# Gates and branches of a mixer computed token-major, half-width inverse levels, attention scores of two head groups in turn

## Chip, cores, metric

One core of one Trainium2 chip runs the whole program. The metric is the device time of one execution in microseconds (us); lower is better. Nothing is shared with another core.

## The reference, cut to what matters

The input is 256 tokens of 1024 features; two layers follow one another. Each layer is a feed-forward part, a mixer and a second feed-forward part, each with a residual. The mixer projects the normed input by `w_in` into the inputs of three branches and into gate logits, runs the three branches, and sums them, gated:

```python
(c_q, c_kv, k_rope, g_q, g_k, g_v, g_b, g_a, g_z, m_qkv, gate_logits) = split_cols(h @ w_in[l], IN_SPLITS)
o_mla = mla_branch(...)      # latent attention, 8 heads of 96, causal
o_gdn = gdn_branch(...)      # gated delta rule, 4 heads of 128, chunked, with a triangular solve
o_moba = moba_branch(...)    # attention, 8 heads of 64, causal (one block of 256 keys)
branches = jnp.stack([o_mla, o_gdn, o_moba], axis=2)            # each 512 wide
up = jnp.einsum('bsnw,nwd->bsnd', branches, w_branch[l])         # 3 x (256 x 1024)
gates = jax.nn.sigmoid(gate_logits.reshape(b, s, N_BRANCH, D_MODEL))
x = x + jnp.sum(gates * up, axis=2) @ w_out[l]
```

All data are float32. Matrix products with weights are done in three passes: weights and inputs are split into a high part (`wh`, `xh`, a rounded type) and a low part (`wl`, `xl`), and xh*wh, xh*wl and xl*wh are summed. The attention and delta-rule products run in plain float32; in the profile such a matmul has two records on TensorE.

## The kernel before

**Steps.** The work with weights is cut into steps of at most 512 KB of weights. A step's weights come by one DMA into a buffer `raw` (`fetch`, L238 to L265; five of them), are split by ScalarE (`wh`, L260) and VectorE (`wl`, L261) in two halves, and are used by TensorE. There are three shapes of step. `chunk` (L267 to L286) is token-major: the input is the stationary operand, 256 rows of weights by 512 columns move; it has two uses, one for each half of the tokens (t = 0 and 1), of six matmuls each, summed into a PSUM bank for each t. `narrow` (L319 to L348) is feature-major: 128x128 pieces of the weights are stationary and all 256 tokens move; a step holds 512 rows by 256 columns, has 24 matmuls of 256 columns into one bank, and a `yield` in its middle. `conv_tile` (L951 on) is feature-major too, with 128 columns.

**The planner's clock.** The program is written out by a planner in Python. `phase` (L1185) walks the steps: use t = 0 of step i and use t = 1 of step i-3 (SKEW) alternate. A joint step (`narrow`, `conv_tile`) does nothing at t = 0 and all of its work at t = 1, in two halves. After each half-step comes a `tick` (L133): every waiting generator in `gens` whose time has come emits its next piece, up to its next `yield n`, which puts it off by n ticks. All that is not a weight step (epilogues, attention, delta rule) lives in such generators. `until` (L142) is used where a step needs a result that isn't emitted yet: it ticks, with no step in between, until the result is there. What is emitted so is then put in order by a scheduler, which mostly keeps this order and sometimes moves a later matmul ahead of one that it thinks not ready.

**The order.** In the mixer, `ORDER` (L42) is a string of 67 letters, one for each step after the four first ones: M is a step of the second attention's inputs, L of the latent attention's, C a convolution tile of the delta rule, Z its output gate, G a step of the gates (24), B one of the branches' products (12). Branches come in the order 0 (latent attention), 2 (second attention), 1 (delta rule). After them come eight steps of `w_out`.

**Gates and branches.** `gates` (L1137) makes four column pieces of 256 for each branch n; each is two steps (1024 rows), and its epilogue (`epi_gate`, L1118) is one tanh on ScalarE. `branch` (L1160) makes four pieces of one step (512 rows); its epilogue `epi_b` (L1145) is one VectorE operation out of PSUM (L1148), for the second and third branch one more that adds to the sum (L1152), and after the last branch a split of the sum (L1156: L358 on ScalarE, L359 on VectorE) straight into the operands of `w_out`, since it is feature-major already. The first piece of each branch calls `until` for its attention or delta rule, at the use, which for a joint step is at t = 1.

**Attention.** `attention` (L560) follows a plan. `s0` and `s1` spawn `scores` (L569) for a group of heads, the first 128 queries of four heads or the second 128 of two: matmuls into one bank (L574), a mask (L576), a maximum and a bias on VectorE (L581, L582), an exponential for each head on ScalarE (L586), a reciprocal, and a scaling for each head (L592). `o` (L597) transposes P of two heads (L604 to L606), copies it (L608), and multiplies by the values (L613, L614), one head into partitions 0 to 63, the other into 64 to 127 of one bank. In the second attention a head's queries and keys lie on 64 partitions, even heads on 0 to 63, odd ones on 64 to 127. `hold` (L118) lets at most two such score banks be in flight; PSUM has eight banks, two for transposes (`tp`) and six for the rest.

**Delta rule.** `gdn` (L628) waits for convolution tiles. `invert` (L739) makes a 128x128 matrix for each of four heads and two token halves c, sends it to DRAM (L759); `small` (L701) reads its 16x16 diagonal blocks back, inverts them on VectorE (L721, L724), writes them to DRAM (L732) and reads them as block-diagonal matrices `zz` (L735). Then `invert` transposes them (L669), and two levels join neighbouring blocks: a matmul with a masked matrix (L772), a copy (L774), a matmul with the transposed inverse (L780), and an addition on VectorE into the even blocks' columns alone (L783). `solve` (L813) ends the branch (L864).

## Time and profile before

| | |
|---|---|
| median of 3 runs | 1350.1 us (1348.01 to 1353.65) |
| the profiled execution | 1350.52 us, of which the span of the profile is 1348.5 us |
| TensorE busy | 1320.3 us, 98% of the span |
| VectorE, ScalarE, GpSimd busy | 70%, 58%, 9% |
| DMA | 231.25 MB, mean 171 GB/s |

The first mixer lies at about 204 to 496 us of the span, the second one at 870 to 1162. In the profile PE is TensorE's matmuls, PEld its weight loads, DVE is VectorE, ACT is ScalarE, POOL is GpSimd, SP is the engine whose queue issues all DMAs. A row of a timeline or a group shows the line of the kernel, the operation, what it writes and what it reads (`acc<-q,wh`: into a bank `acc` from tiles `q` and `wh`), with shapes. The duration of a matmul reaches from its start to the end of its last result; matmuls overlap, so that the distance between two starts is shorter than the duration.

### The profile page before, as it was taken

Reading aid. Unit: us, or ns where it says so; the run is one execution under the profiler, and the core shown is the slowest. Engines: PE = TensorE matmul, PEld = TensorE weight load, DVE = VectorE, ACT = ScalarE, POOL = GpSimd, SP = SyncE. Lnnn points to the kernel's source line nnn. Section 1 sums busy time; section 2 is a strip of 40 time slices with the busy share of each in tenths; the row PEclk is TensorE's granted clock in tenths of the full one; section 3 lists DMA queues with packets and bytes.
Section 4 is the critical chain, followed back from the end, with each engine's and each line's share of the span. In section 5 each row is a group of like instructions: output and inputs, shape, how many; then the busy total and the mean of one; then the engine's idle time right before and its main releaser. Section 6 shows DMA issues by size and latency. Waiting matters only on the chain.

```text
span 1348.5 us, 21398 instructions
## 1 busy us (share of the span) xinstructions
PE 1320.3 (98%) x7786; PEld 1150.3 (85%) x7786; DVE 937.4 (70%) x1890; ACT 786.9 (58%) x1783; POOL 117.9 (9%) x157
## 2 busy tenths in 40 slices
PE   6999999999999999999999999999999999999998
PEld 5888888788999988888888888887889999888887
DVE  6777558888457677775577775588865576777752
ACT  6666447776654556664466654487656544666642
POOL 0010003711101000000000000044120000000000
PEclk9999999999999999999999999999999999999999
DMA  8765566566343657665666556555553445666551
GB/s 277 233 221 185 177 181 167 145 169 176 103 131 110 188 156 218 188 189 176 197 196 194 185 176 184 158 173 160 153 157 99 139 127 171 187 188 189 191 184 62
DMA packets 207561, 231.25 MB, mean 171 GB/s; under 512 B 15616, under 2 KB 166112, under 8 KB 207456
## 3 DMA queue, kind: packets, MB, share of 16 engines
q1 hardware_dynamic: 207456, 229.89, 56.4%
q8 instruction: 61, 1.00, 0.3%
q14 instruction: 44, 0.36, 0.1%
HBM read 227.11 MB, written 2.75 MB: 170 GB/s over the span
## 4 chain that ended last, share of the span: by engine, by line
PE 92%; DVE 3%; ACT 2%; POOL 1%; DMA 1%; issue 1%; SPq 0%; DVEq 0%; ACTq 0%; POOLq 0%
PE acc L309 22%; PE acc L311 11%; PE acc L280 10%; PE acc L282 10%; PE acc L281 10%; PE acc L340 5%; PE acc L341 5%; PE acc L342 5%; PE acc L965 3%; PE pm L574 2%; PE acc L966 1%; ACT wh L260 1%; DMA raw<-in_ffa_w_in 1%; DVE wl L261 1%; PE tp L370 1%; PE pm L613 1%
## 5 line engine op out<-in xcount | busy, mean ns | idle before, releaser
L261 DVE TENSOR_TENSOR wl<-raw,wh 128x512 fp32r<-128x512 f32 (+1 forms) x844 | 563.2, 687 | 265.7 <-ACT wh L260 265.4
L260 ACT CAST wh<-raw 128x512 fp32r<-128x512 f32 (+1 forms) x844 | 497.2, 619 | 389.7 <-issue 147.4
L309 PE MATMUL acc<-q,wh 128*128 128x512 f32 x1280 | 449.3, 396 | 0.0
L311 PE MATMUL acc<-q,wl 128*128 128x256 f32 x1280 | 359.2, 281 | 0.0
L309 PEld LDWEIGHTS acc<-q,wh 128*128 128x128 f32 x1280 | 240.1, 188 | 55.8
L280 PE MATMUL acc<-wh,q 128*128 128x512 f32 (+2 forms) x656 | 259.1, 395 | 1.4 <-ACT q L358 1.4
L282 PE MATMUL acc<-wh,q 128*128 128x512 f32 (+2 forms) x656 | 256.1, 390 | 0.0
L281 PE MATMUL acc<-wl,q 128*128 128x512 f32 (+2 forms) x656 | 255.5, 390 | 0.0
L311 PEld LDWEIGHTS acc<-q,wl 128*128 128x128 f32 x1280 | 242.4, 189 | 0.5
L340 PE MATMUL acc<-q,wh 128*128 128x256 f32 x576 | 168.3, 292 | 0.0
L341 PE MATMUL acc<-q,wh 128*128 128x256 f32 x576 | 163.2, 283 | 0.4 <-DVE q L359 0.4
L342 PE MATMUL acc<-q,wl 128*128 128x256 f32 x576 | 163.0, 283 | 0.0
L280 PEld LDWEIGHTS acc<-wh,q 128*128 128x128 f32 x656 | 123.9, 189 | 26.3 <-ACT q L358 2.4
L282 PEld LDWEIGHTS acc<-wh,q 128*128 128x128 f32 x656 | 123.5, 188 | 26.2 <-DVE q L359 2.2
L281 PEld LDWEIGHTS acc<-wl,q 128*128 128x128 f32 x656 | 123.8, 189 | 21.7
L340 PEld LDWEIGHTS acc<-q,wh 128*128 128x128 f32 x576 | 110.3, 192 | 1.8 <-issue 1.0
L341 PEld LDWEIGHTS acc<-q,wh 128*128 128x128 f32 x576 | 110.3, 191 | 1.2 <-DVE q L359 0.8
L342 PEld LDWEIGHTS acc<-q,wl 128*128 128x128 f32 x576 | 110.1, 191 | 0.1
L965 PE MATMUL acc<-q,wh 128*128 128x512 f32 x192 | 70.5, 406 | 0.0
L486 DVE TENSOR_TENSOR d<-d,acc 128x256 f32<-128x256 f32 x160 | 66.5, 416 | 5.3 <-ACT d L484 5.3
L484 ACT COPY d<-acc 128x256 f32<-128x256 f32 x160 | 58.8, 368 | 18.9 <-PE acc L311 18.8
L392 POOL TENSOR_TENSOR s<-s,mhalf 128x1 f32<-128x1 f32 x12 | 8.3, 691 | 634.3 <-DVE s L385 634.3
(203 smaller groups left out, 1280.9 us busy)
## 6 DMA issues: line engine op xcount, KB each, us to landing
raw<-in_w_in SPq DMA_DIRECT2D x104, 512.0 KB
raw<-in_ffa_w_in SPq DMA_DIRECT2D x88, 512.0 KB
raw<-in_ffb_w_in SPq DMA_DIRECT2D x88, 512.0 KB
raw<-in_ffa_w_out SPq DMA_DIRECT2D x44, 512.0 KB
raw<-in_ffb_w_out SPq DMA_DIRECT2D x44, 512.0 KB
raw<-in_w_branch SPq DMA_DIRECT2D x24, 512.0 KB
raw<-in_w_out SPq DMA_DIRECT2D x16, 512.0 KB
raw<-in_w_in SPq DMA_DIRECT2D x8, 416.0 KB
```

The source lines that it names most:

```text
L260: nc.scalar.copy(s.wh[:, v], s.raw[:, v])
L261: nc.vector.tensor_sub(s.wl[:, v], s.raw[:, v], s.wh[:, v].bitcast(F32))
L280: mm(o, xh, wh[:, j, :], start=(k == 0), stop=False)
L281: mm(o, xh, wl[:, j, :], start=False, stop=False)
L282: mm(o, xl, wh[:, j, :], start=False, stop=(k == nk - 1))
L309: mm(ps.rearrange("p (s c) -> p s c", s=2), wh[:, k, v], x2, start=(g == 0 and k == 0), stop=False, skip_group_check=True)
L311: mm(ps[:, 0:256], wl[:, k, v], x2[:, 0, :], start=False, stop=last, skip_group_check=True)
L340: mm(o, wh[:, k, v], xh, start=(g == 0 and c == 0 and k == 0), stop=False, skip_group_check=True)
L341: mm(o, wh[:, k, v], xl, start=False, stop=False, skip_group_check=True)
L342: mm(o, wl[:, k, v], xh, start=False, stop=(4 * g + k == nk - 1), skip_group_check=True)
L486: nc.vector.tensor_tensor(dst, dst, ps[:, 0:256], op=OP.add)
L965: mm(p, wh[:, k, :], self.X[k // 2][:, k % 2], start=(k == 0), stop=False, skip_group_check=True)
```

## The change

Gates and branch products become `chunk` steps: for each branch two column pieces of 512, token-major; `narrow` goes. Their epilogues run once for each column piece c and token half t, and after the last branch the sum is transposed (four 128x128 transposes into a `tp` bank) and split in two parts. The `until` of a branch moves to `before`, which is called ahead of use t = 0. `ORDER` is a new string: G and B in whole pieces, the four Z together. The two levels of the inverse multiply the even blocks' columns alone (64 of 128 for each head). `scores` takes several groups: the second attention gives it two at a time, of even and odd heads, holds both banks, and issues the matmuls of the two groups in turn; the plan has seven entries, not ten. `outputs` issues both heads' first products and then both second ones.

```diff
@@ -39,7 +39,7 @@
 Y_ATT, Y_INV, Y_DMA, LAG, START, G_AHEAD = 3, 3, 8, 2, 40, 20
-ORDER = "MMLMMLMMCMLMCMCMCGMMCCCGCZZCGGZZBGBGGCGGBGGBGGGCCGGBGBGBGGGGGBBBGBB"
+ORDER = "MMLMMLMMCMLMCMCMCMMCCCGGGGCZZZZCBBGGGGCBBGGGGCCBBGGGGBBGGGGBBGGGGBB"
@@ -115,11 +115,11 @@
         self.held["acc"] += 1
         return self.ps.tile([128, 512], F32, name=self.nm("acc"), tag="bank", bufs=BANKS)
-    def hold(self):
-
-        while self.held["pm"] >= BANKS - 4:
-            yield 1
-        self.held["pm"] += 1
+    def hold(self, n=1):
+
+        while self.held["pm"] + n > BANKS - 4:
+            yield 1
+        self.held["pm"] += n
     def done(self, what):
         self.held[what] -= 1
@@ -316,37 +316,6 @@
-    def narrow(self, w, nk, a0, both, epi, before=None):
...
@@ -566,32 +535,42 @@
         P0, P1 = {}, {}
         left = [len(plan)]
-        def scores(hs, n, w, q0, dst):
...
+        def scores(groups, n, w, q0, dst):
             t = q0 // 128
+            yield from self.hold(len(groups))
+            banks = [self.pm().rearrange("p (h k) -> p h k", h=n) for _ in groups]
+            for i in range(n):
+                for hs, ps in zip(groups, banks):
+                    mm(ps[:, i, :], getq(hs[i])[:, q0:q0 + 128], getk(hs[i])[:, 0:w], start=(i == 0), stop=False,
+                       skip_group_check=True)
+            for ps in banks:
+                mm(ps[:, :, w - 128:w], self.identb, self.maskA[:, None, :].to_broadcast([128, n, 128]), start=False,
+                   stop=True, skip_group_check=True)
+            made = []
+            for hs, ps in zip(groups, banks):
+                rqs = rq[t][:, hs[0]:hs[-1] + 1:hs[1] - hs[0]]
+                mx, nb = (self.sm(4)[:, 0:n] for _ in range(2))
+                nc.vector.tensor_reduce(mx, ps, axis=AX.X, op=OP.max)
+                nc.vector.scalar_tensor_tensor(nb, mx, -1.0, rqs, op0=OP.mult, op1=OP.mult)
+                made.append((hs, ps, rqs, nb))
+            yield 1
+            soft = []
+            for hs, ps, rqs, nb in made:
+                P, sm = self.b2().rearrange("p (h k) -> p h k", h=n), self.sm(4)[:, 0:n]
+                for h in range(n):
+                    nc.scalar.activation(P[:, h, :], ps[:, h, :], AF.Exp, scale=rqs[:, h:h + 1], bias=nb[:, h:h + 1],
+                                         accum_out=sm[:, h:h + 1])
+                self.done("pm")
+                soft.append((hs, P, sm))
+            yield 1
+            for hs, P, sm in soft:
+                rs = self.sm(4)[:, 0:n]
+                nc.vector.reciprocal(rs, sm)
+                for h in range(n):
+                    nc.scalar.activation(P[:, h, :], P[:, h, :], AF.Copy, scale=rs[:, h:h + 1])
+                for i, h in enumerate(hs):
+                    dst[h] = P[:, i, :]
             left[0] -= 1
         def outputs(hs):
@@ -608,17 +587,18 @@
                 nc.scalar.copy(PT[-1][:, 0:384], pt[:, 0:3, :].rearrange("p j k -> p (j k)"))
             yield 1
             o = self.pm()[:, 0:256]
-            for i, h in enumerate(hs):
-                ov = o[64 * i:64 * i + 64, :]
-                mm(ov, getv(0, h), PT[i][:, 0:256], start=True, stop=False, skip_group_check=True)
-                mm(ov[:, 128:256], getv(1, h), PT[i][:, 256:384], start=False, stop=True, skip_group_check=True)
+            halves = [(o[64 * i:64 * i + 64, :], h, PT[i]) for i, h in enumerate(hs)]
+            for ov, h, pt in halves:
+                mm(ov, getv(0, h), pt[:, 0:256], start=True, stop=False, skip_group_check=True)
+            for ov, h, pt in halves:
+                mm(ov[:, 128:256], getv(1, h), pt[:, 256:384], start=False, stop=True, skip_group_check=True)
             k = hs[0] // 2
             self.split(oT[k // 2][:, k % 2, 0, :], oT[k // 2][:, k % 2, 1, :], o)
             left[0] -= 1
-        for what, hs in plan:
+        for what, *hs in plan:
             if what == "o":
-                yield from outputs(hs)
+                yield from outputs(hs[0])
             else:
                 self.spawn(scores(hs, 4, 128, 0, P0) if what == "s0" else scores(hs, 2, 256, 128, P1))
             yield Y_ATT
@@ -767,20 +747,22 @@
             back(zz[:, :, 0, :], zz[:, :, 1, :])
             yield 1
             for l in range(LEVELS - 1):
-                p = v4(self.pm())
+
+                even = lambda z: z.rearrange("p h (m s b) -> p h m s b", s=2, b=16 << l)[:, :, :, 0, :]
+                half = lambda z: z[:, 0:256].rearrange("p (h c) -> p h c", h=H)
+                v = even(zz[:, :, 0, :])
+                p = half(self.pm())
                 for h in range(H):
-                    mm(p[:, h, :], cm[:, h, :], zz[:, h, 0, :], start=True, stop=True)
-                t1 = v4(self.b2())
+                    mm(p[:, h, :], cm[:, h, :], v[:, h], start=True, stop=True)
+                t1 = half(self.b2())
                 nc.scalar.copy(t1, p)
                 cm = v4(self.b2())
                 nc.gpsimd.tensor_tensor(cm, nk, brow(self.lev[l + 1]), op=OP.mult)
                 yield Y_INV
-                p = v4(self.pm())
+                p = half(self.pm())
                 for h in range(H):
                     mm(p[:, h, :], zz[:, h, 1, :], t1[:, h, :], start=True, stop=True)
-                even = lambda z: z.rearrange("p h (m s b) -> p h m s b", s=2, b=16 << l)[:, :, :, 0, :]
-                v = even(zz[:, :, 0, :])
-                nc.vector.tensor_tensor(v, even(p), v, op=OP.add)
+                nc.vector.tensor_tensor(v, p.rearrange("p h (m b) -> p h m b", b=16 << l), v, op=OP.add)
                 yield Y_INV
                 back(zz[:, :, 0, :], zz[:, :, 1, :])
@@ -1075,8 +1057,8 @@
             d["oT", 2] = [newT() for _ in range(2)]
             sl = lambda z, h: z[64 * (h % 2):64 * (h % 2) + 64, h // 2, :]
             yield from self.attention(
-                [("s0", (0, 2, 4, 6)), ("s0", (1, 3, 5, 7)), ("s1", (0, 2)), ("s1", (1, 3)), ("o", (0, 1)),
-                 ("s1", (4, 6)), ("o", (2, 3)), ("s1", (5, 7)), ("o", (4, 5)), ("o", (6, 7))],
+                [("s0", (0, 2, 4, 6), (1, 3, 5, 7)), ("s1", (0, 2), (1, 3)), ("o", (0, 1)), ("s1", (4, 6), (5, 7)),
+                 ("o", (2, 3)), ("o", (4, 5)), ("o", (6, 7))],
                 lambda h: sl(d["mT", 0], h), lambda h: sl(d["mT", 1], h),
                 lambda tt, h: d["mv", tt][:, h, :], [d["mr", 0], d["mr", 1]], d["oT", 2])
             d["o", 2] = True
@@ -1115,10 +1097,10 @@
             moba += self.chunk(self.wcols(w_in, [(a0, a0 + 512)]), 8, 512, xget, epi_m(i))
-        def epi_gate(n, j):
-            def f(ps):
-                d["gate", n, j] = self.b2()
-                nc.scalar.activation(d["gate", n, j], ps, AF.Tanh, scale=0.5)
+        def epi_gate(n, c):
+            def f(t, ps):
+                d["gate", n, c, t] = self.b2()
+                nc.scalar.activation(d["gate", n, c, t], ps, AF.Tanh, scale=0.5)
                 self.done("acc")
                 return
                 yield
@@ -1136,15 +1118,16 @@
         def gates(n):
             r = []
-            for j in range(4):
-                r += self.narrow(w_in, 8, GATE + n * D + j * 256, self.xboth, epi_gate(n, j))
+            for c in range(2):
+                a0 = GATE + n * D + c * 512
+                r += self.chunk(self.wcols(w_in, [(a0, a0 + 512)]), 8, 512, xget, epi_gate(n, c))
             return r
         order = (0, 2, 1)
-        def epi_b(n, j):
-            def f(ps):
-                v, s = d["gate", n, j], d["gate", order[0], j]
+        def epi_b(n, c):
+            def f(t, ps):
+                v, s = d["gate", n, c, t], d["gate", order[0], c, t]
                 nc.vector.scalar_tensor_tensor(v, v, 1.0, ps, op0=OP.add, op1=OP.mult)
                 self.done("acc")
                 if n == order[0]:
@@ -1152,22 +1135,28 @@
                 nc.vector.tensor_tensor(s, s, v, op=OP.add)
                 if n == order[-1]:
                     yield 1
-                    q = newT()
-                    self.split(q[:, :, 0, :], q[:, :, 1, :], s.rearrange("p (k c) -> p k c", k=2))
-                    d["aT", j] = q
+                    if t == 0:
+                        d["aq", c] = [newT() for _ in range(2)]
+                    self.transpose_split(s, 4, [(q[:, :, 0, t * 128:(t + 1) * 128], q[:, :, 1, t * 128:(t + 1) * 128],
+                                                 2 * i, 2 * i + 2) for i, q in enumerate(d["aq", c])])
+                    d["aT", c, t] = True
             return f
         def branch(n):
             r = []
-            both = lambda k: d["oT", n][k // 2][:, k % 2]
-            for j in range(4):
-                r += self.narrow(ins["w_branch"][l, n], 4, j * 256, both, epi_b(n, j),
-                                before=(lambda: self.until(lambda: ("o", n) in d)) if j == 0 else None)
+
+            def oget(t, k):
+                q = d["oT", n][k // 2]
+                return q[:, k % 2, 0, t * 128:(t + 1) * 128], q[:, k % 2, 1, t * 128:(t + 1) * 128]
+            for c in range(2):
+                w = self.wcols(ins["w_branch"][l, n], [(c * 512, c * 512 + 512)])
+                r += self.chunk(w, 4, 512, oget, epi_b(n, c),
+                                before=(lambda: self.until(lambda: ("o", n) in d)) if c == 0 else None)
             return r
         def aget(t, k):
-            self.until(lambda: ("aT", k // 2) in d)
-            q = d["aT", k // 2]
+            self.until(lambda: ("aT", k // 4, t) in d)
+            q = d["aq", k // 4][k // 2 % 2]
             return q[:, k % 2, 0, t * 128:(t + 1) * 128], q[:, k % 2, 1, t * 128:(t + 1) * 128]
         z = self.chunk(self.wcols(w_in, [(G_Z, G_Z + 512)]), 8, 512, xget, epi_z)
```

## Rows read from the trace of the kernel before

**Rows 1.** The page's head: busy time, share of the span and instructions of the engines; and the chain that ended last, by engine.

```profile
PE 1320.3 (98%) x7786; PEld 1150.3 (85%) x7786; DVE 937.4 (70%) x1890; ACT 786.9 (58%) x1783; POOL 117.9 (9%) x157
...
PE 92%; DVE 3%; ACT 2%; POOL 1%; DMA 1%; issue 1%; SPq 0%; DVEq 0%; ACTq 0%; POOLq 0%
```

**Rows 2.** Busy time by stretch of the first mixer: the stretch and its length, then busy time and (x) instructions of PE, PEld, DVE, ACT and POOL, TensorE's granted clock, the share of the DMA engines, GB/s.

```profile
204.00:320.00 116.00, 113.68 (x648) 97.35 (x646) 103.07 (x286) 85.50 (x244) 42.13 (x58) 1.00 0.61 167
300.00:320.00 20.00, 19.97 (x128) 17.38 (x126) 19.33 (x62) 14.53 (x35) 0.00 (x0) 1.00 0.57 159
320.00:340.00 20.00, 17.54 (x129) 15.19 (x129) 11.84 (x23) 9.83 (x20) 7.21 (x5) 1.00 0.56 162
340.00:420.00 80.00, 80.00 (x636) 73.66 (x634) 45.61 (x91) 48.64 (x119) 2.81 (x4) 1.00 0.42 119
```

**Rows 3.** Groups by line, whole span, forms kept apart: busy time in all, mean ns of one, and idle time before them. L340 stands for the three lines of `narrow`, L280 for the three of `chunk`.

```profile
L280 PE MATMUL acc<-wh,q 128*128 128x512 f32 x608 | 242.2, 398 | 1.4 <-ACT q L358 1.4
...
L340 PE MATMUL acc<-q,wh 128*128 128x256 f32 x576 | 168.3, 292 | 0.0
```

**Rows 4.** TensorE's timeline in a stretch of `chunk` steps alone (the end of a feed-forward part): the start and the duration in us. The first and the last of 187 consecutive matmuls.

```profile
149.62 0.39 PE L280 MATMUL acc<-wh,q 128*128 128x512 f32 x1
...
191.78 0.39 PE L280 MATMUL acc<-wh,q 128*128 128x512 f32 x1
```

**Rows 5.** The same view at the end of the first mixer: the first and the last of 144 consecutive matmuls of `narrow`, then the first and the last of 12 consecutive ones of `chunk`.

```profile
444.81 0.28 PE L340 MATMUL acc<-q,wh 128*128 128x256 f32 x1
...
461.97 0.28 PE L342 MATMUL acc<-q,wl 128*128 128x256 f32 x1
...
474.57 0.40 PE L280 MATMUL acc<-wh,q 128*128 128x512 f32 x1
...
477.09 0.39 PE L282 MATMUL acc<-wh,q 128*128 128x512 f32 x1
```

**Rows 6.** TensorE's timeline at small float32 work; rows that follow one another on one line are merged (xcount, from the first start to the last end). Sixteen matmuls of one column and what follows them; eight of 128 columns; four transposes and what follows them.

```profile
318.90 1.84 PE L683 MATMUL tp<-cst,q 128*128 128x1 f32 x16
320.67 0.66 PE L613 MATMUL pm<-d,d 128*64 128x256 f32 x4
...
333.76 1.06 PE L772 MATMUL pm<-q,d 128*128 128x128 f32 x8
...
433.52 0.60 PE L864 MATMUL tp<-ident,d 128*128 128x128 f32 x4
433.87 0.36 PE L340 MATMUL acc<-q,wh 128*128 128x256 f32 x1
```

**Rows 7.** TensorE's timeline around attention: outputs in the slow form (303.08 to 304.25), a group of four heads of the second attention (340.43 to 341.55), one of two heads (356.27 to 357.37), outputs in the form of most (376.51 to 377.32). Each has with it the start of what follows.

```profile
303.08 0.81 PE L613 MATMUL pm<-d,d 128*64 128x256 f32 x3
...
304.25 0.50 PE L965 MATMUL acc<-q,wh 128*128 128x512 f32 x1
...
340.43 1.16 PE L574 MATMUL pm<-q,q 64*128 64x128 f32 x8
...
341.55 0.47 PE L340 MATMUL acc<-q,wh 128*128 128x256 f32 x1
...
356.27 1.13 PE L574 MATMUL pm<-q,q 64*128 64x256 f32 x4
...
357.37 0.36 PE L340 MATMUL acc<-q,wh 128*128 128x256 f32 x1
...
376.51 0.66 PE L613 MATMUL pm<-d,d 128*64 128x256 f32 x4
...
377.32 0.39 PE L340 MATMUL acc<-q,wh 128*128 128x256 f32 x1
```

**Rows 8.** SP's timeline: the issue of the eight writes of the small inverses to DRAM, and of the first read of them.

```profile
325.61 3.38 SPq L732 DMA_DIRECT2D zd<-d  x8
329.83 0.61 SPq L735 DMA_DIRECT2D q<-zd  x1
```

**Rows 9.** TensorE's timeline where it first uses what was read, for both token halves; in brackets the idle time before it and what ended it.

```profile
333.29 0.63 PE L669 MATMUL tp<-ident,q 128*128 128x128 f32 x4 [1.41 <-DMA q<-zd]
...
335.70 0.63 PE L669 MATMUL tp<-ident,q 128*128 128x128 f32 x4 [0.89 <-DMA q<-zd]
```

**Rows 10.** ScalarE's timeline: from the first exponential of a group of four heads to what follows its last scaling, and the same for a group of two.

```profile
343.42 0.46 ACT L586 ACTIVATE d<-pm,s,s 128x128 f32<-128x128 f32 x1 [1.87 <-DVE s L582]
...
346.72 1.13 ACT L260 CAST wh<-raw 128x512 fp32r<-128x512 f32 x2
...
359.13 0.56 ACT L586 ACTIVATE d<-pm,s,s 128x256 f32<-128x256 f32 x1 [0.87 <-DVE s L582]
...
361.38 1.12 ACT L260 CAST wh<-raw 128x512 fp32r<-128x512 f32 x2
```

**Rows 11.** Two views. From the list of waits of the whole span, that of TensorE's transposes of the second attention's keys on VectorE: us in total, times, the longest. And VectorE's timeline behind the last matmul of a branch piece, from L1148 to L1152, which ends 0.69 us after its start.

```profile
PE tp L997 <- DVE d L1108: 4.2, 4, 1.4
...
470.51 0.69 DVE L1148 SCALAR_TENSOR_TENSOR d<-d,acc 128x512 f32<-128x512 f32 x1 [1.99 <-PE acc L342]
...
471.72 0.69 DVE L1152 TENSOR_TENSOR d<-d,d 128x512 f32<-128x512 f32 x1
```

**Rows 12.** TensorE's timeline at the program's start, two of its first matmuls.

```profile
13.23 0.63 PE L281 MATMUL acc<-wl,q 128*128 128x512 f32 x1
13.65 0.63 PE L282 MATMUL acc<-wh,q 128*128 128x512 f32 x1
```

More of the change, by code (lines that the diff above doesn't have):

```diff
@@ L315, in use @@
                         yield
-            return Step(load, use, joint=True)
-        return [step(g) for g in range(nk // 4)]
-    def narrow(self, w, nk, a0, both, epi, before=None):
-        acc = []
-        def step(g):
-            def load():
-                return [w[g * 512:(g + 1) * 512, a0:a0 + 256].rearrange("(k p) n -> p k n", p=128)], 4, 256
-            def use(wh, wl):
-                if g == 0:
-                    if before:
-                        before()
-                    acc.append(self.acc())
-                ps = acc[0]
-                mm = self.nc.tensor.matmul
-                for c in range(2):
-                    o = ps[:, c * 256:(c + 1) * 256]
-                    v = slice(c * 128, (c + 1) * 128)
-                    for k in range(4):
-                        x2 = both(4 * g + k)
-                        xh, xl = x2[:, 0, :], x2[:, 1, :]
-                        mm(o, wh[:, k, v], xh, start=(g == 0 and c == 0 and k == 0), stop=False, skip_group_check=True)
-                        mm(o, wh[:, k, v], xl, start=False, stop=False, skip_group_check=True)
-                        mm(o, wl[:, k, v], xh, start=False, stop=(4 * g + k == nk - 1), skip_group_check=True)
-                    if c == 0:
-                        yield
-                if 4 * g + 4 == nk:
-                    self.spawn(epi(ps))
             return Step(load, use, joint=True)
@@ L610, in outputs @@
             o = self.pm()[:, 0:256]
-            for i, h in enumerate(hs):
-                ov = o[64 * i:64 * i + 64, :]
-                mm(ov, getv(0, h), PT[i][:, 0:256], start=True, stop=False, skip_group_check=True)
-                mm(ov[:, 128:256], getv(1, h), PT[i][:, 256:384], start=False, stop=True, skip_group_check=True)
+            halves = [(o[64 * i:64 * i + 64, :], h, PT[i]) for i, h in enumerate(hs)]
[3 more added lines that the diff above has]
+                mm(ov[:, 128:256], getv(1, h), pt[:, 256:384], start=False, stop=True, skip_group_check=True)
             k = hs[0] // 2
```

21 lines of the change are left out of this document (removed).

## The prediction

> **What bounds the kernel now.** I read the page's head first: TensorE has work in 98% of the span, and the chain that ended last is 92% TensorE [rows 1]. The reader is to see that little is idle, so a gain must come from TensorE needing less time per step, not from a stall removed. Next the stretches of the first mixer: TensorE idles 2.3 us of 116, then 2.5 of 20, then nothing for 80, while VectorE is at 103 of 116 in the first and far from full afterwards [rows 2]. So the mixer is TensorE's, with VectorE close behind it early on.
>
> The trap is in the groups by line: a 256-column matmul of `narrow` has a mean of 292 ns and a 512-column one of `chunk` 398 ns [rows 3]. By these durations 1728 narrow ones (576 on each of three lines) against 864 wide ones would be worth some 150 us. But matmuls overlap; what counts is the distance of their starts. The wide ones start 42.16 us apart over 186 intervals, 0.2267 us each [rows 4]. The narrow ones start 17.16 us apart over 143 intervals, 0.1200 us each, and wide ones inside the mixer's end 2.52 us over 11, 0.2291 us [rows 5]. So two narrow matmuls cost 0.240 us and one wide 0.227 to 0.229.
>
> **The change part by part.** The sum is made against the profiled execution, 1350.5 us (span 1348.5, 2.0 around it), 0.4 above the median of the runs.
>
> *Gates and branches.* Columns and steps stay as they are (36 steps a layer, 512 KB each), matmuls halve. 1728 x 0.1200 = 207.4 us go; 864 x 0.228 = 197.0 come: -10.4, with ends -11.5 (0.2267) and -9.5 (0.2291). All of it is on the path. The tanh and the two VectorE operations keep their number and shape. Each load has half as many rows, twice as long, on the same queue.
>
> By the Trainium skill, page "TensorE: Matmul & The Clock Gate", section "Back-to-back issue gap", a stream of load-and-matmul pairs sustains 131 ns at 512 columns and 81 ns at 128. With some 98 ns at 256 columns, an estimate between these two, this part would be worth 1728 x 0.098 - 864 x 0.131 = 56 us; the rows show 0.227 and 0.120 us here, and the sum goes by them.
>
> *The sum transposed.* New on TensorE: four transposes for each of two column halves and two token halves, 8 sets in both layers. A set of four takes 0.35 us from its start to the next matmul and 0.60 to the end of its last result [rows 6]: +2.8 to +4.8, taken +3.2, nearer to the first, since the next matmul overlaps. The 512-wide split becomes two 256-wide ones out of PSUM, on engines with room at that stage: nothing.
>
> *Scores of both halves.* Only the second attention (64 rows per head) is paired. One group of four heads occupies TensorE for 1.12 us, one of two heads for 1.10 [rows 7]; a layer has two and four of them, 6.6 us, both layers 13.3. After the change heads on rows 0 to 63 and 64 to 127 alternate, into different banks. No row shows two row halves at once. The nearest are the outputs, which already alternate column halves in most cases: eight records, four of them 256 columns wide, in 0.81 us, against 1.17 where they don't [rows 7]. By these two groups overlap almost wholly: -6.4. If two weight loads can't overlap, the 128-column group, which is bound by its loads (next part), keeps its time: -4.6. If nothing overlaps: 0. I take -5.2, near the outputs' rows. A loss, a drain at each change of half, is what the alternating outputs speak against.
>
> *Outputs.* Their new order is what the trace mostly has already; two of sixteen are in the slow form: 2 x 0.36 = -0.7.
>
> *Inverse levels.* Sixteen one-column matmuls take 1.77 us, 0.111 us each, and eight 128-column ones are no slower per record [rows 6]: with a full weight load, fewer columns buy nothing. 0 on TensorE. ScalarE's copies get shorter, off the path; at most they shorten a wait inside the chain.
>
> *The order.* A half-step is one pass of the planner's clock. I counted yields against the old and the new order string. In the old one the first branch step (B of branch 0) has to wait 2 passes for the first attention, that of branch 2 waits 3, that of branch 1 none; in the new one 5, 2 and none. In such passes mixer work is emitted with no step between. The delta rule's end thus stays hidden, and the second attention, 10 passes shorter, is in time. Exposed are three places.
>
> (1) The round trip of the 16x16 inverses through DRAM: write issued at 325.61, read at 329.83, TensorE starts on it at 333.29, 7.7 us later, after 1.41 us of idleness, and once more after 0.89 [rows 8, 9]. Between the write and the first use lie 7 half-steps now and 3 then: 4 x 1.38 = 5.5 us less cover. Against it: the first score statistics and the K-Q products (32 records of 0.111, 3.6 us) stay or come into the gap, two convolution epilogues leave the window in which VectorE (19 of 20 us busy there) computes those inverses, so that the write should leave earlier, and the second use gets a half-step before it. SP holds weight loads behind that read, with three steps already split. I take +0.25 a layer, ends -1 and +5.4 (7.7 fully exposed, less 2.3 paid today).
>
> (2) The second attention's softmax bunches up on ScalarE. A group of four heads takes 3.3 us there, one of two 2.2 [rows 10]; before the first transposes of P that is 11 us, now spread over 13 half-steps, then over 7. With splits and copies of the inverse ScalarE has 16 to 18 us to do there, TensorE some 17. A PSUM bank is also held longer behind that bunch. Ends 0 and +3 a layer, taken +0.5.
>
> (3) The new transposes stand one half-step (1.38 us) behind the matmul they depend on, and wait for two VectorE operations with a split between them: from 470.51 to 472.41 [rows 11], 0.6 us too long, 8 times, +5 at most. The nearest wait of that kind, also one pass behind, took 4.2 us over 4 [rows 11], but on a full VectorE. Against it, matmuls of a later step can be ahead of them in the queue. Taken +1.5.
>
> Sum: -10.4 - 5.2 - 0.7 + 3.2 + 0.5 + 1.0 + 1.5 = -10.1. 1350.5 - 10.1 = 1340.4, and as a median 1340.
>
> **The rivals.** *Waits eat it.* If places (1) to (3) cost 10 us instead of 3, or 5 and the row halves don't overlap, the time is 1345 to 1349. For it: VectorE's load early in the mixer and the bunch on ScalarE. Against it: the trace's 80 us after 340 without any idleness.
>
> *No wait at all and full overlap.* -11.5 - 6.4 - 0.7 + 2.8 - 2 = -17.8: 1333.
>
> *Slower: the round trip lies bare and TensorE's clock falls.* Place: between the last output of the first attention and the first transposes of the inverse. At its full price (1) is +5.4 a layer. In this trace TensorE, after 9.3 us without work, ran its first matmuls 0.43 us apart [rows 12], half the pace of [rows 4], that is at the lower of its two levels, 1.2 GHz, until 17.5 us. As much again in each layer, some 5 us at half pace, is 2.5 more. It decides from 5 us of cost a layer on. With (2) and (3) at their upper middle, 3 a layer, 1350.5 - 13.1 + 2 x (5.4 + 2.5 + 3) = 1359. Against it: after the 1.41 us of idleness of today the inverse's eight matmuls ran at full pace [rows 6].
>
> The Trainium skill, page "TensorE: Matmul & The Clock Gate", section "HAM oscillation — how this bites in real kernels", says that a long enough gap between bursts sends the array back to half rate; that is this rival's second half, and only the start of this trace shows it.
>
> *The change doesn't do what it says:* row halves run one after the other. Then 1345.6, within the first rival.
>
> **How the numbers follow.** About 0.5% (6.75 us) is what a measurement of this kernel can tell from no change: faster is below 1343.4, slower above 1356.9. Forecast, 1334 to 1343: 0.55. No waits, below 1334: 0.12. Waits eat it, 1343.4 to 1356.9, mostly 1345 to 1350: 0.24. Bare round trip: 0.09. So faster 0.67, same 0.24, slower 0.09. The range of 8 in 10 reaches from just under the best sum to past the first rival: 1331 to 1351. It leaves out the slower rival and some of each tail.
>
> **What would show each step.** Wide matmuls at 0.227 to 0.229 us from start to start in the mixer's last 60 us. Records of the paired scores within 0.02 us of each other, and a pair of groups in 1.2 to 1.4 us. The inverse's matmuls still 0.11 us apart. TensorE's wait for the inverses' read under 2.5 us a layer, with the last outputs of the first attention right before it and no step between. A wait of under 0.5 us before the new transposes. Wrong it would be if the idle time of the stretch around the first attention's end or of the second attention's start grew by over 5 us a layer, if matmuls in the mixer started at half the pace of [rows 4], or if the wide matmuls there were 0.24 us apart.

## The result and the profile after

The changed kernel takes 1344.4 us (median of 7 runs, 1343.5 to 1345.1) against 1350.5 us before (1348.0 to 1354.2): a ratio of 0.9947, 95% interval [0.9934, 0.9960]. Its profiled span is 1342.5 us. That is 6 us less, where 10 were forecast. In the kernel after, `transpose_split` is at L339, the paired scores at L545 and L548, the transposes of P at L583 to L585, the score statistics at L663 (the delta rule's sums of squares of its queries, sixteen one-column matmuls) with their square at L658, the inverses' read at L715 and its transposes at L649.

First the mixer's length. I count a mixer from the start of the last wide matmul ahead of its input's transposes to that of the last one ahead of the next normalisation's. TensorE's timeline of the kernel after, start and duration in us:

```profile
199.33 0.39 PE L280 MATMUL acc<-wh,q 128*128 128x512 f32 x1
200.18 0.33 PE L339 MATMUL tp<-ident,d 128*128 128x128 f32 x1 [0.46 <-DVE d L365]
...
487.83 0.39 PE L281 MATMUL acc<-wl,q 128*128 128x512 f32 x1
488.84 0.30 PE L339 MATMUL tp<-ident,d 128*128 128x128 f32 x1 [0.62 <-DVE d L365]
```

487.83 - 199.33 = 288.5 us, and 288.5 in the second layer. Before, the same marks are 292.1 and 292.0 apart; in the first layer:

```profile
200.62 0.39 PE L280 MATMUL acc<-wh,q 128*128 128x512 f32 x1
...
492.72 0.39 PE L281 MATMUL acc<-wl,q 128*128 128x512 f32 x1
```

So the mixers give 7.1 us together. The rest of the span lies in stretches that the diff doesn't touch (see the end). Each length is read from the one profiled execution of its kernel.

Then the parts. The same view at the end of the first mixer: the first and the last of 57 consecutive wide matmuls, a set of the new transposes and what follows it; further up the first level of an inverse and a pair of score groups with their masks.

```profile
335.27 1.00 PE L756 MATMUL pm<-q,d 128*128 128x64 f32 x8
336.11 0.61 PE L649 MATMUL tp<-ident,q 128*128 128x128 f32 x4
...
337.48 1.16 PE L545 MATMUL pm<-q,q 64*128 64x128 f32 x16
338.58 0.61 PE L548 MATMUL pm<-cb 128*128 128x512 bf16 x2
338.83 0.58 PE L280 MATMUL acc<-wh,q 128*128 128x512 f32 x1
...
433.20 0.48 PE L280 MATMUL acc<-wh,q 128*128 128x512 f32 x1
...
445.99 0.39 PE L282 MATMUL acc<-wh,q 128*128 128x512 f32 x1
446.44 0.63 PE L339 MATMUL tp<-ident,d 128*128 128x128 f32 x4
446.82 0.48 PE L280 MATMUL acc<-wh,q 128*128 128x512 f32 x1
```

The wide ones start 12.79 us apart over 56 intervals, 0.228 each, where [rows 5] has 0.229. Eight inverse records of 64 columns still take 0.84 us to the next instruction, 0.105 each, near the 0.111 of [rows 6]: half the columns bought nothing. Sixteen score records of two groups take 1.10 us to their masks where one group of eight took 1.12 with its mask [rows 7]: the halves overlap wholly. With both masks the pair takes 1.35 us.

What grew is the end of the first attention. Busy time by stretch (PE, PEld, DVE, ACT, POOL, then TensorE's granted clock, the DMA share and GB/s):

```profile
322.00:324.00 2.00, 1.99 (x12) 1.40 (x10) 2.00 (x5) 0.01 (x1) 1.10 (x1) 1.00 0.36 103
324.00:326.00 2.00, 0.00 (x0) 0.00 (x0) 2.00 (x4) 1.98 (x4) 0.19 (x1) 1.00 0.95 321
326.00:328.00 2.00, 1.56 (x8) 1.56 (x8) 0.30 (x1) 0.39 (x1) 0.00 (x0) 0.61 0.96 324
328.00:330.00 2.00, 2.00 (x11) 2.00 (x12) 0.00 (x0) 0.00 (x0) 0.00 (x0) 0.50 1.02 386
330.00:332.00 2.00, 2.00 (x10) 1.32 (x10) 0.17 (x1) 0.96 (x2) 0.46 (x1) 0.50 0.46 176
332.00:334.00 2.00, 2.00 (x13) 1.50 (x12) 0.10 (x1) 0.37 (x1) 0.81 (x1) 0.68 0.00 0
```

TensorE has nothing to do from 324 on, and then runs at half of its pace (0.50, 1.2 GHz) until past 332. The timeline of all engines says why; in brackets the idle time before and what ended it:

```profile
320.67 1.95 PE L676 MATMUL pm<-q,q 128*128 128x128 f32 x16
...
322.37 0.48 PE L280 MATMUL acc<-wh,q 128*128 128x512 f32 x1
...
323.60 0.39 PE L282 MATMUL acc<-wh,q 128*128 128x512 f32 x1
...
324.02 1.14 ACT L260 CAST wh<-raw 128x512 fp32r<-128x512 f32 x2 [2.02 <-PE acc L282]
325.07 0.37 ACT L327 CAST q<-pm 128x256 fp32r<-128x256 f32 x1
325.33 1.06 ACT L658 ACTIVATE q<-q 128x1024 f32<-128x1024 f32 x1
...
326.44 3.57 PE L663 MATMUL tp<-cst,q 128*128 128x1 f32 x16 [2.46 <-ACT q L658]
...
329.88 0.45 PE L583 MATMUL tp<-ident,d 128*128 128x128 f32 x1
...
333.38 0.65 PE L649 MATMUL tp<-ident,q 128*128 128x128 f32 x4
```

In the passes of the branch's wait only six wide matmuls stand between the K-Q products (L676) and the score statistics (L663). ScalarE's queue has a weight split ahead of the square that the statistics need, and the split waits for the buffer that the sixth matmul frees. So split, copy and square follow TensorE one after another, 2.46 us. The inverses' transposes (L649) come right behind the outputs and wait for nothing. Their read is not late; SP's timeline of the writes and the first read:

```profile
316.64 3.75 SPq L712 DMA_DIRECT2D zd<-d  x8
321.65 0.61 SPq L715 DMA_DIRECT2D q<-zd  x1
```

The write left at 316.64 instead of 325.61 [rows 8].

### The profile page after: what moved, and what is told of

It is laid out like the page before. It is cut to its first block, busy times and chain, and to the rows that moved or that the text cites. A ratio compares the mean times of both kernels' runs of the same rounds, so it can differ in the third digit from the quotient of the medians.

```text
span 1342.5 us, 19777 instructions
## 1 busy us (share of the span) xinstructions
PE 1314.6 (98%) x6954; PEld 1104.1 (82%) x6954; DVE 940.3 (70%) x1898; ACT 787.4 (59%) x1791; POOL 116.8 (9%) x157
## 4 chain that ended last, share of the span: by engine, by line
PE 92%; DVE 3%; ACT 1%; POOL 1%; DMA 1%; issue 1%; SPq 0%; DVEq 0%; ACTq 0%; POOLq 0%
PE acc L309 22%; PE acc L280 15%; PE acc L282 15%; PE acc L281 15%; PE acc L311 11%; PE acc L947 3%; PE acc L948 1%; PE pm L545 1%; PE tp L339 1%; DMA raw<-in_ffa_w_in 1%; PE pm L592 1%; ACT wh L260 1%; DVE wl L261 1%; POOL s L334 1%; PE tp L979 1%
## 5 line engine op out<-in xcount | busy, mean ns | idle before, releaser
L280 PE MATMUL acc<-wh,q 128*128 128x512 f32 (+2 forms) x944 | 376.0, 398 | 1.4 <-ACT q L327 1.4
L282 PE MATMUL acc<-wh,q 128*128 128x512 f32 (+2 forms) x944 | 368.5, 390 | 0.0
L281 PE MATMUL acc<-wl,q 128*128 128x512 f32 (+2 forms) x944 | 368.3, 390 | 0.0
L311 PE MATMUL acc<-q,wl 128*128 128x256 f32 x1280 | 358.7, 280 | 0.0
L309 PEld LDWEIGHTS acc<-q,wh 128*128 128x128 f32 x1280 | 240.2, 188 | 57.5
L311 PEld LDWEIGHTS acc<-q,wl 128*128 128x128 f32 x1280 | 241.7, 189 | 0.5
L280 PEld LDWEIGHTS acc<-wh,q 128*128 128x128 f32 x944 | 177.7, 188 | 37.9 <-ACT q L327 1.8
L282 PEld LDWEIGHTS acc<-wh,q 128*128 128x128 f32 x944 | 177.5, 188 | 37.6 <-DVE q L328 1.7
L281 PEld LDWEIGHTS acc<-wl,q 128*128 128x128 f32 x944 | 177.8, 188 | 31.2
L948 PE MATMUL acc<-q,wl 128*128 128x256 f32 x192 | 53.9, 281 | 0.0
L327 ACT CAST q<-tp 128x256 fp32r<-128x256 f32 x80 | 28.3, 369 | 32.3 <-PE tp L339 21.2
L947 PEld LDWEIGHTS acc<-q,wh 128*128 128x128 f32 x192 | 36.1, 188 | 8.8 <-issue 0.7
L562 ACT ACTIVATE d<-pm,s,s 128x128 f32<-128x128 f32 (+1 forms) x64 | 31.9, 510 | 17.2 <-DVE s L555 17.2
L334 POOL TENSOR_TENSOR s<-s,mhalf 128x4 f32<-128x4 f32 (+2 forms) x32 | 37.2, 1165 | 2.5
L948 PEld LDWEIGHTS acc<-q,wl 128*128 128x128 f32 x192 | 36.3, 189 | 0.7
```

Source lines behind the costliest of these rows:

```text
L280: mm(o, xh, wh[:, j, :], start=(k == 0), stop=False)
L281: mm(o, xh, wl[:, j, :], start=False, stop=False)
L282: mm(o, xl, wh[:, j, :], start=False, stop=(k == nk - 1))
L309: mm(ps.rearrange("p (s c) -> p s c", s=2), wh[:, k, v], x2, start=(g == 0 and k == 0), stop=False, skip_group_check=True)
L311: mm(ps[:, 0:256], wl[:, k, v], x2[:, 0, :], start=False, stop=last, skip_group_check=True)
L334: g.tensor_tensor(out, out, self.mhalf[:, 0:out.shape[-1]], op=OP.pow)
```

## Experiments

Times are medians; each ratio is to the kernel before, run beside it. "Mixers" are the lengths defined above, first and second layer. A "pass" is one round of a branch's wait, by the count of yields.

**Another order string, nothing else.**

```diff
-ORDER = "MMLMMLMMCMLMCMCMCMMCCCGGGGCZZZZCBBGGGGCBBGGGGCCBBGGGGBBGGGGBBGGGGBB"
+ORDER = "MMLMMLMMCMLMCMCMCMMCCCGGGGCZZZZCGGGGBBCBBGGGGCCGGGGBBBBGGGGBBGGGGBB"
```

> The changed kernel with another order string and nothing else: the B steps of each branch stand behind the ticks in which its attention ends, so that no branch step calls for rounds without a step between (counted from the yields: 0, 0 and 0 rounds for branches 0, 2 and 1, against 5, 2 and 0). Theory S: the changed kernel fell short of the forecast because of one place in each mixer, 2.46 us of TensorE idleness before the statistics' matmuls (waiting for ScalarE's square) and the half clock behind it, some 3 us; with matmul steps in between both go, and the time falls by 8 to 11 us to 1333 to 1336, with no slice of the granted clock below 1. Theory W: the wide matmuls or their epilogues in the mixer cost more than the 0.227 to 0.229 us of the forecast; then the order gives under 3 us, 1341 or more.

1337.5 us, 0.9903 [0.9888, 0.9917]; mixers 284.3 and 284.2, 4.3 us each below the kernel after. The same place in its timeline:

```profile
321.08 1.95 PE L676 MATMUL pm<-q,q 128*128 128x128 f32 x16
322.78 0.48 PE L280 MATMUL acc<-wh,q 128*128 128x512 f32 x1
...
328.32 1.85 PE L663 MATMUL tp<-cst,q 128*128 128x1 f32 x16
330.03 0.31 PE L583 MATMUL tp<-ident,d 128*128 128x128 f32 x1
```

24 wide matmuls now stand where six stood, the statistics wait for nothing, and they take 1.71 us to the next instruction instead of 3.44. By the mixers the order of the change kept back 8.6 us of what the edits are worth, by the times 7, and this version beats both kernels. The time is 1.5 us above the first theory's range; the second theory falls, and the granted clock stays at 1.00 in both mixers.

**The square on GpSimd.**

```diff
-nc.scalar.activation(sq, sil(0), AF.Square)
+nc.gpsimd.tensor_tensor(sq, sil(0), sil(0), op=OP.mult)
```

> The changed kernel with the square for the delta rule's statistics on GpSimd, not on ScalarE, so that it no longer stands behind two weight splits there. Theory S: the idleness before the statistics' matmuls goes, and if nothing else waits at the same place the half clock goes with it: 1334 to 1339. Rival: the next item in TensorE's queue, the first attention's last outputs, waits for ScalarE's copies behind the same two splits, so that the idle time only moves: within 2 us of the changed kernel, with the clock low as before. Theory W: no difference.

1345.2 us, 0.9956 [0.9944, 0.9968]; mixers 287.4 and 288.3. The timeline:

```profile
321.89 2.34 POOL L658 TENSOR_TENSOR q<-q 128x1024 f32<-128x1024 f32 x1
...
324.87 1.84 PE L663 MATMUL tp<-cst,q 128*128 128x1 f32 x16
...
329.92 0.47 PE L583 MATMUL tp<-ident,d 128*128 128x128 f32 x1 [2.82 <-DVE s L666]
```

Theory S, 1334 to 1339, is wrong. The statistics come at once, and the instruction behind them waits 2.82 us instead: their PSUM tile is read by VectorE (L666), which stands behind weight splits. The idle time only moves, as in the rival, but to VectorE's small step and not to ScalarE's copies. So it isn't the square as such: in both runs a small step behind weight splits, once on ScalarE and once on VectorE, came late while TensorE had six wide matmuls queued.

**Scores and outputs alone** (the kernel before with the paired scores, the reordered outputs and the plan of the second attention).

```diff
-            yield from self.hold()
+            yield from self.hold(len(groups))
...
-                [("s0", (0, 2, 4, 6)), ("s0", (1, 3, 5, 7)), ("s1", (0, 2)), ("s1", (1, 3)), ("o", (0, 1)),
+                [("s0", (0, 2, 4, 6), (1, 3, 5, 7)), ("s1", (0, 2), (1, 3)), ("o", (0, 1)), ("s1", (4, 6), (5, 7)),
```

> The kernel before with the scores in turn, the new plan of the second attention and the new order of the outputs alone. If the pairs overlap wholly as in the trace of the changed kernel, TensorE saves 6.3 us, and the rounds without steps before branch 2 go from 3 to 0: 1343 to 1345. If the bunch on ScalarE and the held banks cost what the prediction gave as their end, 3 us a layer, it is 1349 to 1350.

1345.1 us, 0.9954 [0.9939, 0.9969]; mixers 288.0 and 288.0, 4.0 us each below before. That is the first of the two cases. TensorE's wait for the read of the inverses is still there in this run, 5.0 us in four times over both layers.

**Gates, branches and order without the rest** (the kernel after with the attention, its plan and the inverse levels of before).

```diff
-            yield from self.hold(len(groups))
+            yield from self.hold()
...
-                p = half(self.pm())
+                p = v4(self.pm())
```

> The changed kernel with the scores, the plan, the outputs and the inverse levels of the kernel before: gates, branches, epilogues and order alone. TensorE saves 10.4 us and adds 3.2 for the transposes; theory S adds the place at the first attention's end, 2.8 us a layer more than before; and the second attention is again 10 ticks longer, so that branch 2 now calls for 12 rounds without a step, at a price of 0 to 4 us a layer: 1348 to 1357. Theory W without any of the waits: 1345 to 1348, and no low clock.

1359.7 us, 1.0073 [1.0059, 1.0088], 2.7 us above the range; mixers 296.1 and 296.4, 4 us more than before. Beside the wait at the first attention's end it has a second, in the transposes of P of the second attention, which by the count comes too late by 12 passes for its branch:

```profile
395.66 0.27 PE L573 MATMUL tp<-ident,d 128*128 128x128 f32 x1
398.19 0.33 PE L574 MATMUL tp<-ident,d 128*128 128x128 f32 x1 [2.26 <-ACT d L561]
```

**The same with no pass.** The next two separate the order from the form.

```diff
-ORDER = "MMLMMLMMCMLMCMCMCMMCCCGGGGCZZZZCBBGGGGCBBGGGGCCBBGGGGBBGGGGBBGGGGBB"
+ORDER = "MMLMMLMMCMLMCMCMCMMCCCGGGGCZZZZCGGGGBBCBBGGGGCCGGGGGGGGBBBBGGGGBBBB"
```

> The token-major gates and branches with the scores, outputs and inverse levels of before, in an order string in which, counted by yields, no branch step has to wait a pass (the first branch's steps stand two steps later than in the kernel after, the second branch's four later than the first's order would have them). Theory (it is the passes of the wait that cost, not the token-major form): 206.5 instead of 214.9 us for the gates and branches, 2.6 us more for the transposes, and before's two waits of some 2.9 us a layer gone: 1350.6 - 5.8 - 5.8 = 1339, with 1338 to 1343 taken, no idle time of TensorE over 0.7 us between 315 and 345 us nor between 385 and 400. Rival (the token-major form itself slows the mixer, by its transposes or by wide matmuls beside the full VectorE): within 3 us of the same form in the order of after, 1357 to 1361.

1341.8 us, 0.9921 [0.9907, 0.9934]; mixers 286.8 and 286.8: 9.4 us a mixer less than the run before it, by the order string alone. The rival falls.

**The kernel before with no pass.**

```diff
-ORDER = "MMLMMLMMCMLMCMCMCGMMCCCGCZZCGGZZBGBGGCGGBGGBGGGCCGGBGBGBGGGGGBBBGBB"
+ORDER = "MMLMMLMMCMLMCMCMCGMMCCCGCZZCGGZZGGBBGCGGBGGBGGGCCGGGGGBBBGGGGBBBGBB"
```

> The kernel before with nothing but another order string, in which no branch step has to wait a pass (before: 2 passes at the first branch, 3 at the second). Theory (before pays 1.57 + 1.05 + 0.3 us a layer there, because of those passes): the two waits of TensorE for the read of the inverses shrink below 0.5 us together, and the time falls by 3 to 6 us, 1344.5 to 1347.5. Rival (the round trip through DRAM is what before waits for, at whatever order): waits of 2 us a layer or more stay and the time is within 1.5 us of before's, 1349 to 1352.

1344.3 us, 0.9939 [0.9927, 0.9952], 8 us less, a little more than expected; mixers 289.2 and 289.1, 2.9 us each below before. TensorE's timeline where it first uses the inverses, as [rows 9]:

```profile
334.79 0.60 PE L669 MATMUL tp<-ident,q 128*128 128x128 f32 x4
...
337.07 0.60 PE L669 MATMUL tp<-ident,q 128*128 128x128 f32 x4
```

No idle time stands before either. So the waits of [rows 9] hung on the passes too, and moving a few letters of the string is worth as much as the whole change.

**Whole-width inverse levels** in the first experiment's order.

```diff
-                    mm(p[:, h, :], cm[:, h, :], v[:, h], start=True, stop=True)
+                    mm(p[:, h, :], cm[:, h, :], zz[:, h, 0, :], start=True, stop=True)
```

> The kernel after in the order string of the first experiment, with the inverse levels of before (all columns instead of the even blocks'). Theory (with a full weight load a record takes 0.111 us whatever its columns; the shorter copies are off the path): same as the first experiment, 1336 to 1339. Rival (half-width levels shorten the chain copy, multiply, add between the levels, or take columns' time from TensorE): 64 records of 64 columns fewer a layer at 0.0267 us each at most, 1.7 us a layer, or a wait that appears between the levels: 1340 to 1343.

1338.2 us, 0.9890 [0.9874, 0.9906]; mixers 284.5 and 284.3, against 284.3 and 284.2. The narrower levels are worth 0.2 us a mixer at most, nothing that these runs can tell.

**Keys' transposes a pass later** in the first experiment's order (in `epi_m`).

```diff
-                    yield 1
+                    yield 2
                 qk_T(t, y.rearrange("p (k j) d -> p k (j d)", j=2), 128, ("mT", i))
```

> The kernel after in the order string of the first experiment, with the transposes of the second attention's keys one pass later. In the first experiment's trace they are what TensorE still waits for, 2.1 us in all. Theory (a pass of 1.38 us of other work covers most of it): 1 to 2 us less than the first experiment, 1335 to 1337. Rival (what stands behind them, the paired scores, then waits in their place): same as the first experiment, 1337 to 1338.5, with a new wait of TensorE before the second attention's scores.

1336.0 us, 0.9878 [0.9863, 0.9893]; mixers 284.6 and 283.8, so on average no shorter, though the time lies in the theory's range. Of TensorE's waits in the first mixer (in total, times, longest; us) the first experiment has

```profile
PE tp L979 <- DVE d L1090: 2.1, 2, 1.4
```

and this run

```profile
PE tp L979 <- DVE d L1023: 1.5, 2, 1.0
PE pm L592 <- ACT d L587: 0.5, 2, 0.3
```

What the later pass takes from one wait appears at the outputs. The intervals of the two versions overlap.

**How many passes it takes.** Three runs of the kernel after: the second branch's first two steps as in the first experiment, the first branch's at the change's place, then one and two steps later.

```diff
+ORDER = "MMLMMLMMCMLMCMCMCMMCCCGGGGCZZZZCBBGGGGCBBGGGGCCGGGGBBBBGGGGBBGGGGBB"
+ORDER = "MMLMMLMMCMLMCMCMCMMCCCGGGGCZZZZCGBBGGGCBBGGGGCCGGGGBBBBGGGGBBGGGGBB"
+ORDER = "MMLMMLMMCMLMCMCMCMMCCCGGGGCZZZZCGGBBGGCBBGGGGCCGGGGBBBBGGGGBBGGGGBB"
```

> The kernel after with the first branch's steps where the change put them (5 passes of the wait by the count of yields) and only the second branch's first two steps later (0 passes instead of 2). Both orders together gave 4.3 us a mixer. Theory (all of it is at the first attention's end): mixers of 288.0 to 288.7 us as in the kernel after, the 2.5 us wait before the score statistics and the half pace behind it unchanged, the time within 2 us of the kernel after's, 1343 to 1346. Rival (the passes at the second branch cost as well): 1 us a mixer or more less, 287.5 or less, 1340 to 1343.

1346.9 us, 0.9965 [0.9954, 0.9976]; mixers 287.7 and 289.2, on average what the kernel after has; the time is 1 us above the range. The second branch's passes cost nothing that shows.

> As the run before it, with the first branch's steps one step later: 3 passes of the wait by the count instead of 5. Theory (every pass is a half-step of cover less, 4.3 us a mixer for five): the wait before the score statistics, or the one that takes its place, shrinks to about 1 us or less, no half pace behind it, mixers 284.5 to 286.5, the time 1337 to 1341. Rival (any wait there at all costs the whole): 287.5 or more a mixer, 1342 or more.

1337.2 us, 0.9899 [0.9884, 0.9915]; mixers 284.7 and 284.6. Its timeline:

```profile
320.79 1.95 PE L676 MATMUL pm<-q,q 128*128 128x128 f32 x16
322.49 0.48 PE L280 MATMUL acc<-wh,q 128*128 128x512 f32 x1
...
327.80 0.39 PE L282 MATMUL acc<-wh,q 128*128 128x512 f32 x1
328.03 1.85 PE L663 MATMUL tp<-cst,q 128*128 128x1 f32 x16
```

One step later is enough: 24 wide matmuls again, no wait, though three passes are left. So the cost is not so much per pass, as I had it; in these runs it is there or not, according to the work queued ahead of the statistics.

> As the run before it, with the first branch's steps two steps later: 0 passes, the earliest place that has none. Theory (the passes decide, not the distance): as the first experiment, mixers 284 to 285, the time 1334 to 1339, no wait of TensorE over 0.7 us between 315 and 345 us. Rival (the distance counts, since the read of the inverses and ScalarE's work behind the first attention need their time whatever the planner's clock says): a wait of 1 us or more there, mixers 285.5 or more, 1339 to 1342.

1336.9 us, 0.9899 [0.9885, 0.9914]; mixers 283.4 and 283.4. By its interval no faster than the first experiment; its mixers are 0.8 us shorter (see below).

## Why the prediction was right in kind and 4 us off

Right: the direction, the range, and that the gates' gain is 10 us and not 150. But 1344.4 is 1.4 us above the band of 1334 to 1343 that had the chance of 0.55; what came is "waits eat it" (0.24), by a wait at place (1), though not at the price that this rival gives. Of the 4 us that are missing, 3 lie in the mixers (7.1 where the sum has 10.1) and 1 in the stretches around them. The terms, for both layers, from the mixers of the runs (averages of the two; the runs compared also differ in where the branch steps stand):

- *Gates and branches, the new transposes and their wait*: -10.4 + 3.2 + 1.5 = -5.7 in the sum; measured -4.7, from 289.15 (before, no pass) to 286.78 a mixer (token-major, no pass). The pitch is as forecast. The eight sets of transposes are a little dearer: from the start of the matmul ahead to that of the second one behind, less two pitches, they take 0.54 to 0.74 us, 5.0 together (at 446.44 above: 0.45 + 0.38 + 0.32 - 0.46 = 0.69), against 4.7 for set and wait. The other 0.7 us is not accounted for.
- *Scores, outputs and ScalarE's bunch* (place 2): -5.2 - 0.7 + 1.0 = -4.9; measured -4.8, from 286.78 to 284.38 (the run with whole-width levels). That the sum came out is luck, its terms did not. The records of a pair overlap wholly, but the second mask adds to it: the pairs of a layer take 1.35 + 1.22 + 1.21 us to the next instruction where the groups took 6.6, -5.7 in all. The bunch shows no wait of TensorE. The outputs gained nothing: one set of the first attention is in the slow form in each layer still, now 1.44 us where [rows 7] has 1.17:

```profile
301.32 1.07 PE L592 MATMUL pm<-d,d 128*64 128x256 f32 x3
...
302.76 0.50 PE L280 MATMUL acc<-wh,q 128*128 128x512 f32 x1
```

In the first experiment's order a set of the second attention comes in two pieces, 0.58 and 0.79 us instead of 0.80. Both layers' outputs together take 1.1 us more there than in the token-major run with no pass, where -0.7 was forecast. In the order of before the paired scores, outputs and plan gave 4.0 us a mixer and not 2.4, so this term depends on the order in which it is measured.

- *Inverse levels*: 0; measured 0.2 a mixer, from 284.38 to 284.21, not to be told from 0.
- *Place (1), the end of the first attention*: this is the step that failed, "I take +0.25 a layer, ends -1 and +5.4". Measured +1.4 a layer: the kernel after pays 4.3 us there (288.5 to 284.2), the kernel before 2.9 (292.05 to 289.15). That is +2.8 instead of +0.5. That cover would be missing there was right, and no run speaks against the count of the passes; but the prediction watched the inverses' round trip, which came 9 us earlier and was hidden, and took the score statistics for cover. They were what waited, for their own square. The half pace behind the idle time, which stood only in the slower rival, came with it: in rows of the first layer 2.46 us of idleness, 1.73 on the statistics, 0.80 on the six transposes of P (1.50 from the first of them to the outputs, 0.70 in the first experiment) and 0.83 on the outputs (2.00 to the next instruction, 1.17 there).

-4.7 - 4.8 - 0.3 + 2.8 = -7.0, up to rounding the 7.1 of the mixers. It has to be: each term is the step from one run to the next.

The slower rival names the right place and half of its mechanism; its price needed the round trip bare, and no run shows that. The Trainium skill, page "TensorE: Matmul & The Clock Gate", section "HAM oscillation — how this bites in real kernels", has it that a long enough gap between bursts sends the array back to half rate. The kernel after and the runs with the same gap agree (0.50 behind 2.46 us); the 2.26 us of the token-major form alone don't show it (below).

The order with the first branch's steps two places later has mixers 0.8 us shorter than the first experiment's; 0.57 of this is the set of outputs in two pieces, which comes in one piece there, in 0.80 us. What remains open: TensorE's rows at place (1) add up to 5.8 us; with the 0.57 that the first experiment pays for its set in two pieces 5.2 are left, and the mixers differ by 4.3.

## What to carry to other kernels

Where small steps go back and forth between engines, count how much wide work TensorE has queued ahead of each, in us, against the chain that its next operand goes through on the other engines, weight splits ahead of it included. A change of the steps' shape or of the place of a wait moves both, so the old order has to be counted again: here the passes at the first branch went from 2 to 5. Try the order alone on the kernel before as well: here it was worth as much as the change.

## What the runs showed of the hardware

*The clock doesn't follow the length of a gap alone.* Behind the same 2.46 us the kernel after is at half pace at once, while the run with the first branch kept did the first layer's statistics at full pace and fell 2 us later. Its stretches:

```profile
328.00:330.00 2.00, 2.00 (x17) 1.89 (x17) 0.17 (x1) 0.20 (x1) 0.00 (x0) 0.88 0.99 344
330.00:332.00 2.00, 2.00 (x10) 1.13 (x9) 0.00 (x0) 0.76 (x2) 1.26 (x1) 0.50 0.67 259
```

In the second layer it fell within the statistics (2.45 us long) and that mixer is 1.5 us longer. The 2.26 us gap of the token-major form alone (from 395.9 to 398.2) left the clock at 1.00, and so did the stretches of 2 us behind it:

```profile
398.00:400.00 2.00, 1.49 (x10) 1.02 (x10) 0.17 (x1) 1.80 (x5) 0.00 (x0) 1.00 0.34 127
```

*The untouched feed-forward part has two lengths.* From the first mixer's end to the next normalisation it took 185.9 us in before and in the first experiment and 188.05 in the kernel after. The granted clock is 1.00 in all of them from 520 to 550 us. It was 188 in the five token-major kernels whose first branch waits passes (the kernel after, the square on GpSimd, the token-major form alone, the first branch kept, and one step later) and 186 in the other eight. The second such part took 185.2 or 187.4, not in step with the first. I can't say what sets it; it moves a span by 2 us in each, so effects of this size were read from the mixers and not from the times.

*VectorE and GpSimd slow each other down.* Three weight splits on VectorE took 784 ns each in the kernel after (323.5 to 326) and 1801 ns each in the run with the square on GpSimd, whose two operations there were running nearly all the time (groups by line; busy time, mean ns, idle time before). The first row is of the kernel after, the second of that run:

```profile
L261 DVE TENSOR_TENSOR wl<-raw,wh 128x512 fp32r<-128x512 f32 x3 | 2.2, 784 | 0.0
```

```profile
L261 DVE TENSOR_TENSOR wl<-raw,wh 128x512 fp32r<-128x512 f32 x3 | 5.2, 1801 | 0.7 <-ACT wh L260 0.7
```

The last of GpSimd's two operations and the last of the three splits in that run:

```profile
324.19 1.72 POOL L760 TENSOR_TENSOR d<-d,cst 128x512 f32<-128x512 f32 x1
324.70 1.76 DVE L261 TENSOR_TENSOR wl<-raw,wh 128x512 fp32r<-128x512 f32 x1
```

The split ends 0.55 us after GpSimd's operation does, and so do the two ahead of it (2.38 us and 1.27 us long) after the operations that they met. The GpSimd operation took 1.29 us in the kernel after. One of that kernel's three splits met it too and took 0.98 us, the other two 0.68 and 0.69; VectorE's two products that read one operand from PSUM (L678) ran beside it in 0.68 us each, no longer than alone. So the square on GpSimd let the statistics start 1.6 us earlier and cost VectorE 3 us, and the small step behind VectorE's splits is what TensorE then waited for.
